# Loads without a waiting chain go from the sync queue to ScalarE's queue, in a two-layer attention and retention trunk

## The chip, the cores and the metric

The kernel runs on one core of a Trainium2 chip. The metric is the device time of one execution in microseconds; the change is judged by it. The core has five engines that run their own instruction streams and meet at semaphores: TensorE (matmuls; PE in the profile, its weight loads PEld), VectorE (DVE), ScalarE (ACT), GpSimd (POOL) and SyncE (SP), which does nothing here but issue DMAs. Data lie in HBM, in SBUF (128 partitions) and, for matmul results, in PSUM.

## The reference

Two layers over one sequence of 2048 tokens, width 1024, then a last RMS norm. Each layer projects the normed input to eight parts of 512 columns, runs chunked attention (8 heads of 64) and chunkwise retention (4 heads of 128) side by side, gates both, and adds the product with `w_out`:

```python
def hybrid_layer(x, norm_gain, w_in, w_out, rel_bias, cos, sin):
    hn = rms_norm(x, norm_gain)
    aq, ak, av, ag, rq, rk, rv, rg = jnp.split(hn @ w_in, cuts, axis=-1)
    ya = chunked_rel_attention(aq, ak, av, rel_bias)      # own chunk of 64 and 8 before, softmax, relative bias
    yr = chunkwise_retention(rq, rk, rv, cos, sin)        # rotary q and k, decay per head, group RMS norm
    y = jnp.concatenate([ya * silu(ag), yr * silu(rg)], axis=-1)
    return x + y @ w_out

def reference(x, positions, norm_gain, w_in, w_out, rel_bias, final_gain):
    cos, sin = rotary_tables(positions, RET_HEAD_DIM)
    for layer in range(DEPTH):                            # DEPTH = 2
        x = hybrid_layer(x, norm_gain[layer], w_in[layer], w_out[layer], rel_bias[layer], cos, sin)
    return rms_norm(x, final_gain)
```

All of it is in float32; the kernel gets there by splitting each operand of a matmul into a float16 high and a float16 low part and adding three products.

## The kernel before

**Tiling.** The 16 token tiles of 128 form four blocks n of 512. The heads form four groups s, each with two attention heads and one retention head. For each layer l, group s and block n the kernel runs `dense_T` (q, k and the rotary q, k of the group, with features on partitions; four outputs j, 24 matmuls each), then `dense_V` (v, rotary v and gates for four token tiles, 24 matmuls each), and beside the dense work of the next block it runs `attention` and `retention` of this one. After the last group of a layer, `wout` multiplies the concatenated y by `w_out` tile by tile, adds x, and in layer 0 also norms the result for layer 1.

**What is written where.** The context `manual_schedule` covers PE, ScalarE, VectorE and GpSimd: their instructions stand in the order in which the Python code calls them. SyncE is not in it, apart from the first block (`sp_order`, left after the first `dense_V`): there the scheduler puts the DMAs in an order of its own, and may move a load ahead of where it is called. A helper `tc.keep_in_program_order` holds one DMA at its place. Each engine works its own list strictly in order: an instruction that waits for a semaphore holds up all that stand behind it.

**Rounds.** `run` steps the dense generators; a round is one step, 8 matmuls of a dense output. In each round it fires what `later(k, fn)` has put k rounds ahead, steps attention, and pulls steps of background work (`bg`, pushed by `push(gen, steps)`): the weights of the next group. Those steps are:

- `prep_T`: loads four sections of `w_in` (1024 x 128, 512 KB each, `load_sec`, tile `stT`) one section ahead, squares each on ScalarE (`sumsq`), finds a power-of-two scale, and converts it to high and low halves. `prep_V` (tile `stV`) and, between the layers, `prep_V_next` do the same for the other four.
- `prep_Omax`: loads the eight blocks of `w_out` (tiles `stO0m`, `stO1m`) and squares each on ScalarE (L312) to find one common scale. Its loop is short:

```python
        for j in range(KT):
            yield
            m1 = sumsq(st, f"{nm}m{j}", None)
            if j + 1 < KT:
                st = load_sec(w_out[l, :, (j + 1) * P:(j + 2) * P], f"{nm}m{j + 1}")
```

- `prep_O`: loads `w_out` again, four sections for each half (tile `stO`), and converts it (L333).

The tiles of `load_sec` come from the pool `w4` with three buffers, so up to three loads can be under way or waiting for their reader.

**Other loads that the change touches.** `tab_load` brings the two rotary tables of a block (`tabc`, `tabs`, 256 KB each) from DRAM, where `tables` has written them once for each block; GpSimd multiplies with them in `turn`. `Sections` loads the retention mask `msk`. `bias_scratch` spreads a head's relative biases over a DRAM scratch (`toep`), and `bias_tiles` reads it back skewed (`bias`), GpSimd and ScalarE (L584) then finish the tile. `y_load` and `x_load` bring a token tile of y and x for `wout`; `y_squares` (L951) is the first reader of y.

**What stays on the sync queue.** The transposes of attention probabilities (`pT<-pq`, L815), on whose result the products with v wait (L823 to L825); the transposes of y and of the normed rows; the copies of q, k and the swapped halves for the rotary product; the stores of y, x and the output. Between `qk` and `pv` of an attention unit lie: VectorE's add and maximum (L807), ScalarE's exponential (L810) and copy (L812), GpSimd's rest (L813), the transpose.

**PSUM.** The dense outputs use the pool `psD` with two buffers, so the third output waits until the first was copied out: for `dense_V` by ScalarE (L763 to L766), then one round later by VectorE (L769 to L773).

Of the kernel before, what the change touches and what calls it, by code (L numbers as in the profile page):

```python
# [18 lines left out]
P = 128  # L19
EPS = 1e-6  # L20
HALF_PI = 1.5707963267948966
RELW = 767
# [5 lines left out]
def hybrid_trunk(ctx: ExitStack, tc: tile.TileContext, x, pos, gain, gcol, w_in, w_out, rel, fgain,  # L28
# [8 lines left out]
    act, dve, pool, pe, sp = nc.scalar, nc.vector, nc.gpsimd, nc.tensor, nc.sync  # L37
# [30 lines left out]
    y_d = [dp.tile([P, D], F32, tag=f"y_d{t}", name=f"y_d{t}") for t in range(NT)]  # L68
    x_d = [dp.tile([P, D], F32, tag=f"x_d{t}", name=f"x_d{t}") for t in range(NT)]
    tab_d = [dp.tile([2, P, 512], F32, tag=f"tab{n}", name=f"tab{n}") for n in range(NS)]  # L70
# [218 lines left out]
    TSEC = (0, 1, 4, 5)  # L289
    VSEC = (2, 6, 3, 7)  # L290

    def load_sec(src, nm, halves=False):

        v = src.rearrange("(k p) c -> p k c", p=P)
        if not halves:
            st = w4.tile([P, KT, P], F32, tag="w4", name=f"st{nm}")
            sp.dma_start(st, v)
            return [(st, 0, KT)]
        h = KT // 2
        st = [b2.tile([P, 3 - i, 512], F16, tag=("rot2", "rot3")[i], name=f"st{nm}_{i}") for i in range(2)]  # L300
        st = [t_[:, 0:2].rearrange("p a c -> p (a c)").bitcast(F32).rearrange("p (k c) -> p k c", c=P) for t_ in st]
        for i in range(2):
            sp.dma_start(st[i], v[:, i * h:(i + 1) * h, :])
        return [(st[i], i * h, (i + 1) * h) for i in range(2)]

    keep = lambda i: i
# [47 lines left out]
    class Sections:  # L354


        def __init__(self, l, s, g, halves=False):
            g.msk = b2.tile([P, P], F32, tag="msk", name=f"msk{l}_{s}")
            sp.dma_start(g.msk, dmask[:, s, :])
            g.rd, g.s = rdc[:, s:s + 1], s  # L360
            self.l, self.s, self.g, self.halves = l, s, g, halves
            self.nm = f"T{l}_{s}"
            self.sts, self.sq, self.iv, self.sv = [], [None] * 4, [None] * 4, [None] * 4
            g.h = b3.tile([P, 4, KT, P], F16, tag="wh", name=f"wh{self.nm}")
            g.l = b3.tile([P, 4, KT, P], F16, tag="wl", name=f"wl{self.nm}")
# [102 lines left out]
    def prep_V_next(l, g):  # L468

        nm = f"V{l}_0"  # L470
        src = [w_in[l, :, VSEC[j] * 512:VSEC[j] * 512 + P] for j in range(4)]
        sts = [load_sec(src[j], f"{nm}{j}", True) for j in range(2)]
        yield
        for j in (2, 3):
            st = b2.tile([P, KT, P], F32, tag="q", name=f"st{nm}{j}")
            sp.dma_start(st, src[j].rearrange("(k p) c -> p k c", p=P))
            sts.append([(st, 0, KT)])
        yield
        g.vh = b3.tile([P, KT, 512], F16, tag="wh", name=f"wh{nm}")
        g.vl = b3.tile([P, KT, 512], F16, tag="wl", name=f"wl{nm}")  # L480
        hi, lo = ([w_[:, :, j * P:(j + 1) * P] for j in range(4)] for w_ in (g.vh, g.vl))
        m = [lowp(sumsq(sts[j], f"{nm}{j}", hi[j]), f"{nm}{j}") for j in range(2)]
        yield
        m2, m3 = (sumsq(sts[j], f"{nm}{j}", hi[j]) for j in (2, 3))
        dve.tensor_tensor(m2, m2, m3, op=ALU.add)
        m.append(lowp(m2, f"{nm}2"))
        yield
        yield
        iv = [None] * 3
        for j in (2, 0, 1):  # L490
            sv, iv[j] = norm_scale(allsum(m[j], f"{nm}{j}"), f"{nm}{j}", gains[l].i)
            for i in ((2, 3) if j == 2 else (j,)):
                yield from convert(sts[i], hi[i], lo[i], sv)
        yield from V_units(l, 0, g, iv, nm)
        g.vdone = 4
# [37 lines left out]
    toep = {}  # L533
    NH = 4 * 2 * DEPTH
    rel_d = dp.tile([NH, RELW + 1], F32, tag="rel_d", name="rel_d")
# [27 lines left out]
    def bias_scratch(l, s):  # L563
        for hh in range(2):
            h = 2 * s + hh
            d = dp.tile([P * RELW], F32, tag=f"toep{h % 4}", name=f"toep{l}_{h}")
            i = sp.dma_start(d.rearrange("(p w) -> p w", w=RELW),
                             rel_d[l * 8 + h:l * 8 + h + 1, 1:RELW + 1].to_broadcast([P, RELW]))
            if (l, s) != (0, 0):
                tc.keep_in_program_order(i)  # L570
            toep[l, h] = d
        yield

    def bias_tiles(l, s, g):

        g.bias = []
        for hh in range(2):
            h = 2 * s + hh
            bt = b3.tile([P, 640], F32, tag="bias", name=f"bias{l}_{h}")
            sp.dma_start(bt, toep[l, h][127:127 + P * (RELW - 1)].rearrange("(p w) -> p w", w=RELW - 1)[:, 0:640])  # L580
            yield
            pool.memset(bt[64:128, 0:64], NEG)
            pool.memset(bt[0:64, 576:640], NEG)
            act.activation(bt, bt, AF.Copy, scale=g.ci[:, 0:1])  # L584
            g.bias.append(bt)
            yield
# [28 lines left out]
    def dense_T(l, s, n, g, st):  # L615
# [4 lines left out]
        def tab_load():  # L620
            while n not in tab_done:
                pull(1)
            sp.dma_start(st.tabc, tab_d[n][0])
            sp.dma_start(st.tabs, tab_d[n][1])

        first = (l, s, n) == (0, 0, 0)

# [297 lines left out]
    def y_load(l, t):  # L925
        u = St()
        u.nm = f"y{l}_{t}"
        u.t = t
        if t < 8:
            u.y = w4.tile([P, D], F32, tag="w4", name=f"yy{u.nm}")  # L930
        else:
            u.y = b2.tile([P, D], F32, tag="q", name=f"yy{u.nm}")
        sp.dma_start(u.y, y_d[t])
        return u

    def x_load(l, u):
        if l + 1 == DEPTH or u.t < 12:
            f = (hT[l, 0] if l + 1 == DEPTH else hT_of(l + 1, NS - 1))[u.t // 2 % 2].rearrange("p k c -> p (k c)").bitcast(F32)
            u.x = f[:, u.t % 2 * D:(u.t % 2 + 1) * D]
        else:  # L940
            u.x = w4.tile([P, D], F32, tag="w4", name=f"xx{u.nm}")
        sp.dma_start(u.x, x[u.t * P:(u.t + 1) * P, :] if l == 0 else x_d[u.t])

    def y_squares(l, u):
        u.m = b2.tile([P, 1], F32, tag="ym", name=f"ym{u.nm}")
# [213 lines left out]
    def norms_from_input(ts, spaces, rows, tab):  # L1159

        def load(k):
            u = us[k]
            u.x = spaces[k] if spaces else w4.tile([P, D], F32, tag="w4", name=f"xin{u.t}")
            if not spaces:
                sp.dma_start(u.x, x[u.t * P:(u.t + 1) * P, :])

        def sq(k):
            u = us[k]
# [21 lines left out]
        for t in ts:  # L1190
            u = St()
# [172 lines left out]
    for l in range(DEPTH):  # L1364
        gO = [Grp(), Grp()]
        go = Grp()
        for s in range(NSW):
            g = grp(l, s)
            for n in range(NS):
                first = (l, s, n) == (0, 0, 0)  # L1370
                if not first:
                    st = St()
# [4 lines left out]
                if n == 0 and not first:  # L1377
                    bs, bt = bias_scratch(l, s), bias_tiles(l, s, g)
                    later(1, lambda bs=bs: next(bs))
                    for k in (4, 8, 17, 21):  # L1380
                        later(k, lambda bt=bt: next(bt))
                if (l, s) == (0, 0) and 0 < n < NS - 1:
                    if n == 1:
# [30 lines left out]
                run(dense_V(l, s, n, g, st), att, 24 if n == NS - 1 and s < NSW - 1 else 12)  # L1414
                if first:
                    sp_order.__exit__(None, None, None)
                if att[0] is not None:
                    drain(att[0])
                att = [attention(l, s, n, g, st, states.get((l, s, n - 1)))]
# [84 lines left out]
```

## Time and profile before

| | us |
|---|---|
| median of three runs | 2087.54 |
| lowest and highest | 2083.29, 2090.22 |
| the profiled execution | 2084.99 |
| its span, first to last instruction | 2083.2 |
| TensorE busy | 2008.0 (96%) |
| VectorE busy | 1245.1 (60%) |
| ScalarE busy | 1141.9 (55%) |
| GpSimd busy | 679.1 (33%) |

All DMAs that the program issues itself are issued by SyncE: 645504 packets, 311.12 MB, and their time takes 66.0% of the span of 16 DMA engines. Busy time doesn't count the issuing of DMAs or waiting. In the lists of waits a row names the waiting engine, what it was about to write and the line, then what released it, and the total, the number and the longest of these waits. "SPq" rows are the sync queue's own waits. In the timelines a row has start, duration, engine, line, operation, out<-in by the program's names; in square brackets the engine's idle time just before and what ended it. In the list of DMA issues the last number is the median time from issue to landing.

### The profile page before, as it was taken

The page shows a single profiled execution, that of the slowest core. Times are in us where ns is not written, and L with a number is a line of the kernel's source. Part 1 is how long each engine was busy: PE and PEld are TensorE (multiplying, and loading weights), DVE is VectorE, ACT ScalarE, POOL GpSimd, SP SyncE. Part 2 cuts the span into 40 slices and gives each one's busy share as a digit, 9 for nine tenths or more (in the row PEclk, how much of TensorE's full clock was granted, in tenths as well). Part 3 has the DMA queues.
Part 4 walks back from the last instruction along what each step waited for, and adds up shares of the span by engine and source line. Part 5 has one row for each costly group of instructions (what it writes and reads, how often), then busy time and mean ns, then how long its engine had stood idle before and what let it go on. Part 6 is the DMA issues. An engine that isn't in the chain of part 4 may idle for free.

```text
span 2083.2 us, 39398 instructions
## 1 busy us (share of the span) xinstructions
PE 2008.0 (96%) x14014; PEld 1051.6 (50%) x14014; DVE 1245.1 (60%) x3817; ACT 1141.9 (55%) x2530; POOL 679.1 (33%) x701
## 2 busy tenths in 40 slices
PE   6988999999999999998999999999999999999998
PEld 4444555555555555544444555555555555554543
DVE  7776666556556655676653656565655566557643
ACT  7556665456565654554444546554655665446432
POOL 0234343444344434330003343434243334333100
PEclk9999999999999999999999999999999999999999
DMA  8768675547575754799774547555655867548974
GB/s 233 166 152 172 143 164 106 117 112 158 114 185 118 158 141 102 158 227 259 200 188 98 124 102 147 119 124 102 142 119 125 182 145 166 122 102 192 213 197 126
DMA packets 645701, 313.63 MB, mean 151 GB/s; under 512 B 459232, under 2 KB 602080, under 8 KB 645504
## 3 DMA queue, kind: packets, MB, share of 16 engines
q1 hardware_dynamic: 645504, 311.12, 66.0%
q8 instruction: 109, 1.79, 0.4%
q14 instruction: 88, 0.72, 0.1%
HBM read 123.26 MB, written 41.98 MB: 79 GB/s over the span
## 4 chain that ended last, share of the span: by engine, by line
PE 48%; DMA 3%; POOL 1%; issue 1%; DVE 1%; ACT 1%; SPq 0%; POOLq 0%; ACTq 0%; DVEq 0%
PE dT L736 14%; PE dV L755 14%; PE dO L1098 13%; DMA pT<-pq 2%; PE r L857 2%; PE S L804 1%; PE S L803 1%; PE o L823 1%; PE o L824 1%; PE o L825 1%; DMA toep<-rel_d 0%; POOL pq L813 0%; PE ptn L999 0%; DMA stO1m<-in_w_out_dram 0%; ACT sc L810 0%
## 5 line engine op out<-in xcount | busy, mean ns | idle before, releaser
L813 POOL TENSOR_TENSOR pq<-sc,pq 128x640 f16<-128x640 f32 (+4 forms) x256 | 319.9, 1250 | 894.6 <-ACT pq L812 479.7
L810 ACT ACTIVATE sc<-sc,mq,cT 128x640 f32<-128x640 f32 (+4 forms) x256 | 218.5, 853 | 623.8 <-DVE rl L829 324.3
L736 PE MATMUL dT<-hTh,whT 128*128 128x512 f16 x1008 | 350.4, 383 | 5.0 <-DMA hTh<-xa 2.2
L755 PE MATMUL dV<-whV,hTh 128*128 128x512 f16 x1024 | 353.1, 381 | 1.7 <-DVE gt L773 1.3
L755 PE MATMUL dV<-wlV,hTh 128*128 128x512 f16 x1024 | 353.0, 380 | 0.0
L755 PE MATMUL dV<-whV,hTl 128*128 128x512 f16 x1024 | 352.8, 380 | 0.0
L736 PE MATMUL dT<-hTl,whT 128*128 128x512 f16 x1008 | 348.4, 381 | 0.0
L736 PE MATMUL dT<-hTh,wlT 128*128 128x512 f16 x1008 | 348.1, 380 | 0.0
L755 PEld LDWEIGHTS <-hTh 128*128 128x128 f16 x2048 | 196.5, 98 | 217.0 <-DVE gt L773 3.8
L736 PEld LDWEIGHTS <-whT 128*128 128x128 f16 x2016 | 193.1, 98 | 217.8 <-issue 12.9
L807 DVE CUSTOM_DVE_ANT_0 sc<-S,bias 128x640 f32<-128x640 f32 (+4 forms) x256 | 188.4, 736 | 125.3 <-PE S L804 124.6
L1098 PE MATMUL dO<-whO,yhy 128*128 128x512 f16 x512 | 194.6, 380 | 1.0 <-DMA yhy<-hTh 0.8
L1098 PE MATMUL dO<-whO,yly 128*128 128x512 f16 x512 | 194.3, 380 | 1.2 <-DMA yly<-hTl 0.6
L1098 PE MATMUL dO<-wlO,yhy 128*128 128x512 f16 x512 | 194.4, 380 | 0.0
L812 ACT ACTIVATE pq<-sc 128x640 f16<-128x640 f32 (+4 forms) x256 | 171.5, 670 | 8.1
L1098 PEld LDWEIGHTS <-yhy 128*128 128x128 f16 x1024 | 99.8, 98 | 116.1 <-DMA yhy<-hTh 1.3
L755 PEld LDWEIGHTS <-hTl 128*128 128x128 f16 x1024 | 99.2, 98 | 110.8 <-issue 1.7
L736 PEld LDWEIGHTS <-wlT 128*128 128x128 f16 x1008 | 97.5, 98 | 112.9 <-issue 6.2
L823 PE MATMUL o<-v,pT 128*128 128x65 f16 x1120 | 130.5, 194 | 15.6 <-DMA pT<-pq 15.5
L803 PE MATMUL S<-k,q 128*128 128x128 f16 (+3 forms) x592 | 143.6, 269 | 0.0
L823 PEld LDWEIGHTS <-pT 128*128 128x128 f16 x1120 | 106.0, 97 | 53.0 <-DMA pT<-pq 24.4
L804 PE MATMUL S<-k,q 128*128 128x128 f16 (+3 forms) x592 | 131.0, 269 | 0.0
(352 smaller groups left out, 3497.3 us busy)
## 6 DMA issues: line engine op xcount, KB each, us to landing
q<-qq SPq DMA_DIRECT2D x128, 128.0 KB, 2.5
yyy<-y_d SPq DMA_DIRECT2D x32, 512.0 KB, 4.9
stT<-in_w_in_dram SPq DMA_DIRECT2D x27, 512.0 KB, 5.0
stV<-in_w_in_dram SPq DMA_DIRECT2D x26, 512.0 KB, 4.5
k<-kk SPq DMA_DIRECT2D x128, 64.0 KB, 2.0
swp<-rot SPq DMA_DIRECT2D x64, 128.0 KB, 2.7
tabc<-tab SPq DMA_DIRECT2D x32, 256.0 KB, 2.7
tabs<-tab SPq DMA_DIRECT2D x32, 256.0 KB, 3.1
```

The costliest lines, as they stand in the source:

```text
L736: pe.matmul(ps, w_[:, j, kt, :], h_[:, kt, :], start=(m == 0), stop=(m == 23))
L755: pe.matmul(ps, h_[:, kt, a * P:(a + 1) * P], w_[:, kt, :], start=(m == 0), stop=(m == 23))
L803: pe.matmul(o, st.q[:, hx, 0, cs], k_, start=True, stop=False)
L804: pe.matmul(o, st.q[:, hx, 1, cs], k_, start=False, stop=True)
L807: dve.tensor_tensor_reduce(out=v, in0=S[:, 0:w], in1=g.bias[hx][:, 640 - w:640], scale=1.0, scalar=-3.0e38, op0=ALU.add, op1=ALU.max, accu ...
L810: act.activation(v, v, AF.Exp, bias=m[:, 0:1], scale=g.c[:, 0:1])
L812: act.activation(pq[:, 0:w], v, AF.Copy)
L813: pool.tensor_tensor(pq[:, w:2 * w], v, pq[:, 0:w], op=ALU.subtract)
L823: pe.matmul(o[:, 0:65], u.p[:, b, :], v_[:, 0:65], start=(b == 0), stop=False)
L824: pe.matmul(o[:, 0:64], u.p[:, b, :], v_[:, 65:129], start=False, stop=False)
L857: pe.matmul(out_, w_, m_, start=(i == 0), stop=(i + 1 == len(pairs)))
L1098: pe.matmul(ps, h_[:, kt, :], w_[:, kt, :], start=(m == 0), stop=(m == 23))
```

## The change

A new function `bring` issues a DMA on the engine that `bulk["e"]` names. This is the sync engine until the end of the first block's `dense_V`, and ScalarE from there on. The loads of weight sections, masks, Toeplitz scratch, bias tiles, rotary tables, y, x and later input tiles use it: 259 DMAs move to ScalarE's own queue. Because ScalarE is under the manual schedule, they stand there in the order of the calls. The scratch loads lose their `keep_in_program_order`, and the four steps of `bias_tiles` come 6, 10, 19 and 22 rounds after the group's start instead of 4, 8, 17 and 21. The number of instructions and the tiles are the same.

```diff
@@ -289,18 +289,24 @@
     TSEC = (0, 1, 4, 5)
     VSEC = (2, 6, 3, 7)
 
+    bulk = {"e": sp}
+
+    def bring(dst, src):
+
+        return bulk["e"].dma_start(dst, src)
+
     def load_sec(src, nm, halves=False):
 
         v = src.rearrange("(k p) c -> p k c", p=P)
         if not halves:
             st = w4.tile([P, KT, P], F32, tag="w4", name=f"st{nm}")
-            sp.dma_start(st, v)
+            bring(st, v)
             return [(st, 0, KT)]
         h = KT // 2
         st = [b2.tile([P, 3 - i, 512], F16, tag=("rot2", "rot3")[i], name=f"st{nm}_{i}") for i in range(2)]
         st = [t_[:, 0:2].rearrange("p a c -> p (a c)").bitcast(F32).rearrange("p (k c) -> p k c", c=P) for t_ in st]
         for i in range(2):
-            sp.dma_start(st[i], v[:, i * h:(i + 1) * h, :])
+            bring(st[i], v[:, i * h:(i + 1) * h, :])
         return [(st[i], i * h, (i + 1) * h) for i in range(2)]
 
     keep = lambda i: i
@@ -356,7 +362,7 @@
 
         def __init__(self, l, s, g, halves=False):
             g.msk = b2.tile([P, P], F32, tag="msk", name=f"msk{l}_{s}")
-            sp.dma_start(g.msk, dmask[:, s, :])
+            bring(g.msk, dmask[:, s, :])
             g.rd, g.s = rdc[:, s:s + 1], s
             self.l, self.s, self.g, self.halves = l, s, g, halves
             self.nm = f"T{l}_{s}"
@@ -473,7 +479,7 @@
         yield
         for j in (2, 3):
             st = b2.tile([P, KT, P], F32, tag="q", name=f"st{nm}{j}")
-            sp.dma_start(st, src[j].rearrange("(k p) c -> p k c", p=P))
+            bring(st, src[j].rearrange("(k p) c -> p k c", p=P))
             sts.append([(st, 0, KT)])
         yield
         g.vh = b3.tile([P, KT, 512], F16, tag="wh", name=f"wh{nm}")
@@ -564,10 +570,8 @@
         for hh in range(2):
             h = 2 * s + hh
             d = dp.tile([P * RELW], F32, tag=f"toep{h % 4}", name=f"toep{l}_{h}")
-            i = sp.dma_start(d.rearrange("(p w) -> p w", w=RELW),
-                             rel_d[l * 8 + h:l * 8 + h + 1, 1:RELW + 1].to_broadcast([P, RELW]))
-            if (l, s) != (0, 0):
-                tc.keep_in_program_order(i)
+            bring(d.rearrange("(p w) -> p w", w=RELW),
+                  rel_d[l * 8 + h:l * 8 + h + 1, 1:RELW + 1].to_broadcast([P, RELW]))
             toep[l, h] = d
         yield
 
@@ -577,7 +581,7 @@
         for hh in range(2):
             h = 2 * s + hh
             bt = b3.tile([P, 640], F32, tag="bias", name=f"bias{l}_{h}")
-            sp.dma_start(bt, toep[l, h][127:127 + P * (RELW - 1)].rearrange("(p w) -> p w", w=RELW - 1)[:, 0:640])
+            bring(bt, toep[l, h][127:127 + P * (RELW - 1)].rearrange("(p w) -> p w", w=RELW - 1)[:, 0:640])
             yield
             pool.memset(bt[64:128, 0:64], NEG)
             pool.memset(bt[0:64, 576:640], NEG)
@@ -620,8 +624,8 @@
         def tab_load():
             while n not in tab_done:
                 pull(1)
-            sp.dma_start(st.tabc, tab_d[n][0])
-            sp.dma_start(st.tabs, tab_d[n][1])
+            bring(st.tabc, tab_d[n][0])
+            bring(st.tabs, tab_d[n][1])
 
         first = (l, s, n) == (0, 0, 0)
 
@@ -930,7 +934,7 @@
             u.y = w4.tile([P, D], F32, tag="w4", name=f"yy{u.nm}")
         else:
             u.y = b2.tile([P, D], F32, tag="q", name=f"yy{u.nm}")
-        sp.dma_start(u.y, y_d[t])
+        bring(u.y, y_d[t])
         return u
 
     def x_load(l, u):
@@ -939,7 +943,7 @@
             u.x = f[:, u.t % 2 * D:(u.t % 2 + 1) * D]
         else:
             u.x = w4.tile([P, D], F32, tag="w4", name=f"xx{u.nm}")
-        sp.dma_start(u.x, x[u.t * P:(u.t + 1) * P, :] if l == 0 else x_d[u.t])
+        bring(u.x, x[u.t * P:(u.t + 1) * P, :] if l == 0 else x_d[u.t])
 
     def y_squares(l, u):
         u.m = b2.tile([P, 1], F32, tag="ym", name=f"ym{u.nm}")
@@ -1162,7 +1166,7 @@
             u = us[k]
             u.x = spaces[k] if spaces else w4.tile([P, D], F32, tag="w4", name=f"xin{u.t}")
             if not spaces:
-                sp.dma_start(u.x, x[u.t * P:(u.t + 1) * P, :])
+                bring(u.x, x[u.t * P:(u.t + 1) * P, :])
 
         def sq(k):
             u = us[k]
@@ -1377,7 +1381,7 @@
                 if n == 0 and not first:
                     bs, bt = bias_scratch(l, s), bias_tiles(l, s, g)
                     later(1, lambda bs=bs: next(bs))
-                    for k in (4, 8, 17, 21):
+                    for k in (6, 10, 19, 22):
                         later(k, lambda bt=bt: next(bt))
                 if (l, s) == (0, 0) and 0 < n < NS - 1:
                     if n == 1:
@@ -1414,6 +1418,7 @@
                 run(dense_V(l, s, n, g, st), att, 24 if n == NS - 1 and s < NSW - 1 else 12)
                 if first:
                     sp_order.__exit__(None, None, None)
+                    bulk["e"] = act
                 if att[0] is not None:
                     drain(att[0])
                 att = [attention(l, s, n, g, st, states.get((l, s, n - 1)))]
```

## The prediction

> **What bounds the kernel now.** I read the page's head first, then the windows, the waits of TensorE and of the sync queue, the DMA issues, and last the timelines of ScalarE, VectorE and TensorE where the moved loads are used.
>
> ```profile
> span 2083.2 us, 39398 instructions
> PE 2008.0 (96%) x14014; PEld 1051.6 (50%) x14014; DVE 1245.1 (60%) x3817; ACT 1141.9 (55%) x2530; POOL 679.1 (33%) x701
> ```
> ```profile
> 596.00:619.00 23.00, 21.72 (x162) 11.33 (x160) 11.39 (x45) 19.31 (x46) 9.08 (x9) 1.00 0.90 221
> ...
> 856.00:1075.00 219.00, 207.51 (x1223) 102.83 (x1222) 138.78 (x346) 115.33 (x213) 35.89 (x36) 0.99 0.90 218
> ...
> 1614.00:1637.00 23.00, 21.46 (x160) 11.13 (x158) 11.77 (x46) 18.91 (x46) 9.05 (x8) 1.00 0.89 223
> ```
>
> TensorE is the bound: 2008.0 of 2083.2 us, so 75 us is all that any change of queues can win. ScalarE is 55% busy over the span, but the columns of the windows (start:end, length, then busy time of PE, PEld, DVE, ACT, POOL, granted clock, DMA share, GB/s) say that the mean hides something: in the two 23 us in which `prep_Omax` squares W_out, ScalarE is busy for 19.31 and 18.91 us, 84% and 82%. It has some 4 us to spare there. The granted clock is full in these rows and explains nothing.
>
> What the sync queue costs TensorE today:
>
> ```profile
> PEld L823 <- DMA pT<-pq: 24.4, 18, 3.8
> ...
> PE o L823 <- DMA pT<-pq: 15.5, 14, 3.3
> ```
> ```profile
> SPq L580 <- DMA toep<-rel_d: 28.0, 7, 4.6
> ```
> ```profile
> 1480.48 5.18 DMA toep<-rel_d
> 1486.82 8.11 DMA pT<-pq
> ```
>
> TensorE stood 15.5 us, at 14 places, for transposed probabilities. Seven times the sync queue stood for a Toeplitz scratch to land before it could issue the bias load (28.0 us together), with a transpose behind it; the chain of waits shows one such pair, at 1480 and 1487 us. This is what the change can win.
>
> **What is removed from the sync queue: a gain of 13 us.** 259 loads leave it, the waits on the scratch with them. I take nearly the whole 15.5 us of the pT waits as gone, less what transfers still collide: 13. The ends are 0 (a load already under way is on the same DMA engines) and 24, what the weight loads of the same matmuls waited, part of it beside running matmuls.
>
> The Trainium skill, page "DMA: Bandwidth & Descriptors", section "Issuing engines are not separate DMA queues", speaks against more: loads from either queue run on the same 16 DMA engines, and a second issuer saves issue time only. By that rule the gain would come from issue alone, below my 13; no row of before has a load on a second queue, so the trace leaves it open.
>
> **What is added: loads in ScalarE's written order.** The sync engine's order is left to the scheduler, which issues a load as soon as its buffer is free. ScalarE's order is written by hand. So each load now stands where the code calls it, and what ScalarE computes from it stands shortly behind, in the same in-order queue. The issue itself (about 0.4 to 0.5 us, rows below) is small; the landing is not.
>
> ```profile
> 545.94 0.53 SPq L297 DMA_DIRECT2D stO0m<-in_w_out_dram  x1
> ...
> 557.61 0.38 SPq L297 DMA_DIRECT2D stO0m<-in_w_out_dram  x1
> ```
> ```profile
> yyy<-y_d SPq DMA_DIRECT2D x32, 512.0 KB, 4.9
> stT<-in_w_in_dram SPq DMA_DIRECT2D x27, 512.0 KB, 5.0
> stV<-in_w_in_dram SPq DMA_DIRECT2D x26, 512.0 KB, 4.5
> ...
> stO<-in_w_out_dram SPq DMA_DIRECT2D x16, 512.0 KB, 4.9
> ```
> ```profile
> DMA to landing us min/median/max: 4.0/4.9/6.0
> ```
>
> (The last row is that of tile stO0m.) The first W_out block was issued at 545.94 us and squared at 597.22, 51 us later. In the changed program the listing of ScalarE's instructions has it directly ahead of the square.
>
> **prep_Omax, twice: a loss of 46 us.** ScalarE's timeline before:
>
> ```profile
> 597.22 1.04 ACT L312 ACTIVATE stO0m<-stO0m 128x1024 f32<-128x1024 f32 x1
> 598.17 0.19 ACT L312 ACTIVATION_READ_ACCUMULATOR stO0m<-stO0m 128x1 f32 x1
> ...
> 599.26 1.04 ACT L312 ACTIVATE stO0m<-stO0m 128x1024 f32<-128x1024 f32 x1
> ...
> 601.58 1.05 ACT L312 ACTIVATE stO0m<-stO0m 128x1024 f32<-128x1024 f32 x1
> ...
> 604.98 0.92 ACT L810 ACTIVATE sc<-sc,mq,cT 128x640 f32<-128x640 f32 x1 [2.26 <-DVE mq L809]
> ...
> 606.58 1.04 ACT L312 ACTIVATE stO0m<-stO0m 128x1024 f32<-128x1024 f32 x1
> ...
> 608.34 1.04 ACT L312 ACTIVATE stO0m<-stO0m 128x1024 f32<-128x1024 f32 x1
> ...
> 610.49 1.04 ACT L312 ACTIVATE stO0m<-stO0m 128x1024 f32<-128x1024 f32 x1
> ...
> 613.04 0.92 ACT L810 ACTIVATE sc<-sc,mq,cT 128x640 f32<-128x640 f32 x1 [0.90 <-DVE mq L809]
> ...
> 614.64 1.04 ACT L312 ACTIVATE stO0m<-stO0m 128x1024 f32<-128x1024 f32 x1
> ...
> 616.22 1.06 ACT L312 ACTIVATE stO0m<-stO0m 128x1024 f32<-128x1024 f32 x1
> ```
>
> Load j+1 is called right behind square j. Each square with its read-out takes 1.13 us, so the work that lies between a load and its square is the distance of two squares less 1.13 and less idle time: 0, 0.9, 1.2, 1.6, 0.6, 1.0, 2.1 and 0.45 us, 7.9 together. A landing takes 4.0 to 4.9 us; I take 4.5, since a waiting ScalarE leaves the DMA engines emptier. The waits are 8 x 4.5 - 7.9 = 28.1 us per layer. Two things cover some of it: the idle 2.26 + 0.90 in these rows, and TensorE's lead.
>
> ```profile
> 601.99 0.41 DVE L773 SCALAR_TENSOR_TENSOR gt<-gt,dV 128x256 f32<-128x256 f32 x1
> ```
> ```profile
> 604.56 0.38 PE L755 MATMUL dV<-whV,hTh 128*128 128x512 f16 x1
> ```
>
> The PSUM buffer of a `dense_V` block was cleared at 602.40 (VectorE's rest follows ScalarE's copies at once), and TensorE began to fill it again at 604.56: a lead of 2.2 us, which I use as the lead everywhere. Queued behind ScalarE's waiting squares are just these PSUM copies and the exponentials of attention; TensorE has two dense buffers and can go no further. So TensorE loses 28.1 - 3.2 - 2.2 = 22.7 us per layer, 46 in all. With landings of 4.0 it is 37, with 4.9 it is 52.
>
> **The first rotary table for block 1: 6.5 us.**
>
> ```profile
> 95.49 0.59 SPq L128 DMA_DIRECT2D tab<-xa  x1
> ```
> ```profile
> 89.57 1.28 ACT L810 ACT_TABLE_LOAD   x1 [1.59 <-DVE mq L809]
> ```
> ```profile
> tab<-xa SPq DMA_DIRECT2D x8, 64.0 KB, 2.0
> ```
>
> `tab_load` for n = 1 comes right after the switch of queues and reads what the sync queue is still writing. The last write is issued at 95.49 and lands 2.0 later; with two issues ScalarE is free at about 98.3 where it went on at 89.57: 8.7 late, less the lead, 6.5 (0 to 9).
>
> **First sections of prep_T, six times: 11 us.**
>
> ```profile
> 316.05 1.04 ACT L312 ACTIVATE whT<-stT 128x1024 f16<-128x1024 f32 x1
> ...
> 318.06 0.60 ACT L638 ACTIVATE qq<-dT 128x512 f16<-128x512 f32 x1 [0.88 <-PE dT L736]
> ```
>
> Load 0 and its square fall into neighbouring rounds here: 5.0 less 0.88 idle less the lead is 1.9, six times 11 (0 to 20). Sections 1 to 3 are loaded one section ahead, with a whole section's squares, scales and conversions between, and cost nothing.
>
> **The other moved loads.**
>
> ```profile
> 868.36 0.26 ACT L763 ACTIVATE v<-dV 128x128 f16<-128x128 f32 x1
> ...
> 869.49 1.13 ACT L333 ACTIVATE whO<-stO,o_s 128x1024 f16<-128x1024 f32 x1
> ```
> ```profile
> 1980.33 1.15 ACT L226 ACTIVATE hTh<-yyy,sy 128x1024 f16<-128x1024 f32 x1 [4.68 <-DVE iy L145]
> ```
>
> `prep_O`, four groups: between its first load and the conversion stand the copies of one `dense_V` block, 1.1 us (869.49 - 868.36). So 4.9 - 1.1 - 2.2 = 1.6, and half of it again for the third section, which is also called late: 9 us (0 to 20). First loads of `prep_V`, late in five of six groups, with as little between: 4.5 - 1.1 - 2.2 = 1.2 each, 6 us (0 to 15). Output stage of layer 0: `y_load` stands half a tile ahead of its square, and half-sections of layer 1 are issued there too; TensorE is idle for 11.5 us of this stage already (219.00 - 207.51), so it has no lead to give. I take 1 us for each of ten tiles, 10 us (0 to 25). In layer 1's output stage ScalarE idles 4.7 us in each tile and hides it: nothing. x loads are used by VectorE a tile later: nothing. Masks, scratch and bias (its steps come 2, 2, 2 and 1 rounds later, for this distance) keep away from their use: nothing.
>
> **A wait that the change adds.** In the built program every DMA signals one of eight semaphores in turn and waits for the DMA before on the same one. A load on ScalarE therefore waits for one of the sync queue, often issued just before, with ScalarE's whole order behind it. The landings of before say that nearly all of these are over in time; only the table loads of block 0 in six groups stand close behind a store. I take 2 us (0 to 12, that is 2 us for each of the six).
>
> **Sum.** 46 + 6.5 + 11 + 9 + 6 + 10 + 2 - 13 = 77.5 us. The profiled execution took 2085.0 us (span 2083.2), 2.5 under the median of 2087.5; 2085.0 + 77.5 + 2.5 = 2165 us. Lowest terms with the largest gain: 37 - 24 = +13, 2100 us. Highest with no gain: 52 + 9 + 20 + 15 + 20 + 25 + 12 = +153, 2240 us.
>
> **Rivals.**
>
> ```profile
> L815 SPq DMA_TRANSPOSE pT<-pq x256: 1167/1322/4108, 80.8 to 1952.5; - x128
> ```
> ```profile
> L312 ACT ACTIVATE whV<-stV 128x1024 f16<-128x1024 f32 (+1 forms) x30 | 29.6, 986 | 2.1 <-PE dO L1098 2.1
> ```
>
> *Faster:* ScalarE's waits stay under its idle time, and TensorE loses its pT waits. The mechanism is that a wait of up to 5 us falls where ScalarE would wait for VectorE anyway; it decides where ScalarE idles over 5 us per load. For it: 45% idle overall. Against it: the 84% in `prep_Omax`. It would give 2087.5 - 15.5 = 2072. The Trainium skill has a rule on this side (same page, "Queues, rings and completion order"): each DMA engine takes turns between queue rows by packet, so a transpose on one row need not queue behind a load on another. Chance 0.08. *No change,* gain and waits cancelling: 0.03. *Only prep_Omax counts:* the lead covers single waits of 5 us, 2087.5 + 37 - 24 to + 46 - 13, 2100 to 2120: 0.17. *The two queues hold each other up:* ScalarE late makes the sync queue late through the shared semaphores, and loads issue behind a transpose's 1.3 us instead of 0.5. 259 x 0.8 = 207 us of ScalarE's time, half of it on the path, gives 2165 + 100 = 2265: 0.14. *My forecast:* 0.58. The Trainium skill's table "Rules for kernel authors" on the same page says to issue a load early and wait late; this agrees with the forecast, and the 51 us above against none is what it means here.
>
> **Numbers.** Below 0.3% this kernel's runs can't tell a change. Faster 0.08, same 0.03, slower 0.89. The range 2100 to 2240 leaves out the first two and most of the fourth.
>
> **What would show it.** Right: in the windows of `prep_Omax` (by then 23 us longer each) ScalarE's L312 on stO0m waits 3 to 5 us for "DMA stO0m" eight times and TensorE idles for ScalarE or VectorE; idle before L312 on the stV sections, 2.1 us now, at 10 or more; pT waits of the sync queue behind a scratch gone. Wrong: if those L312 waits are there and TensorE is still 96% busy, the lead was deeper than 2.2 us; if L312 waits are absent, loads land sooner than 4 us; if TensorE's new idle time names pT or swp, the queues hold each other up.

## The result, and the profile after

The changed kernel takes 2163.2 us (median of 4 runs, 2161.9 to 2167.7) against 2085.4 us before on the same chip: 1.038 times, 95% interval 1.0345 to 1.0414, so 78 us slower. Forecast were 2165 us, and slower. The profiled execution took 2167.7 us.

The page of the changed kernel: span, busy time, and the queues (packets, MB, share of 16 engines' span). Here q1 carries what SyncE issues, and q10 what ScalarE issues.

```profile
span 2165.9 us, 39273 instructions
...
PE 2028.8 (94%) x14014; PEld 1055.7 (49%) x14014; DVE 1235.5 (57%) x3817; ACT 1144.1 (53%) x2530; POOL 676.3 (31%) x701
...
q1 hardware_dynamic: 530128, 202.52, 46.0%
q10 hardware_dynamic: 115376, 108.60, 18.4%
```

A third of the bytes left the sync queue. TensorE is 20.8 us longer busy with the same 14014 matmuls (2028.8 against 2008.0), and 137 us idle instead of 75. What waits now (engine, line waited at, what ended the wait: us in total, times, longest; L312 of before is L318 here, L333 is L339, L823 is L827, L857 is L861):

```profile
PE r L861 <- ACT dT L865: 28.4, 6, 7.6
...
ACT whO L339 <- DMA stO<-in_w_out_dram: 21.6, 10, 3.9
...
PE r L861 <- DVE dT L869: 21.2, 15, 3.4
...
ACT whT L318 <- DMA stT<-in_w_in_dram: 20.4, 6, 5.0
...
PEld L827 <- DMA pT<-pq: 18.9, 16, 2.9
...
ACT stO1m L318 <- DMA stO1m<-in_w_out_dram: 17.4, 6, 5.8
...
ACT stO0m L318 <- DMA stO0m<-in_w_out_dram: 16.4, 6, 4.8
...
PE o L827 <- DMA pT<-pq: 11.9, 9, 2.4
...
ACT rhy L955 <- DMA yyy<-y_d: 10.4, 6, 6.2
...
ACT L814 <- DMA tab<-xa: 9.3, 1, 9.3
...
ACT whV L318 <- DMA stV<-in_w_in_dram: 7.9, 5, 1.8
```

ScalarE now stands for weights at every place that loads them. TensorE's longest waits have a new name: not a DMA, but the small copy `dT` of retention that stands in ScalarE's order (28.4 us; the waits of before have 4.7 for it). In four of the six, 20 us together, it stands behind a waiting square of `prep_Omax`; the longest, 7.6 us, is behind the wait for the first rotary table. Waits for transposed probabilities fell only from 15.5 to 11.9 us. Windows of the changed kernel over the eight squares of `prep_Omax` in each layer, and over TensorE's work in the output stage of layer 0 (start:end, length, busy PE, PEld, DVE, ACT, POOL, granted clock, DMA share, GB/s):

```profile
612.30:652.00 39.70, 25.08 (x157) 12.65 (x155) 12.70 (x52) 21.42 (x50) 8.40 (x8) 0.83 0.60 134
1677.70:1715.00 37.30, 26.12 (x164) 12.92 (x165) 15.67 (x63) 20.29 (x47) 10.38 (x9) 0.81 0.51 119
```
```profile
929.00:1119.00 190.00, 166.24 (x924) 79.44 (x923) 107.95 (x260) 84.28 (x143) 21.52 (x25) 0.98 1.01 213
```

The work of some 160 matmuls that took 23 us before takes 39.7 and 37.3 us, at a granted clock of 0.83 and 0.81 where it was 1.00. ScalarE's timeline at four of these squares and loads, and TensorE's beside them (start, us, what, and in brackets the idle time before it):

```profile
614.26 1.06 ACT L318 ACTIVATE stO0m<-stO0m 128x1024 f32<-128x1024 f32 x1 [4.85 <-DMA stO0m<-in_w_out_dram]
...
618.59 1.06 ACT L318 ACTIVATE stO0m<-stO0m 128x1024 f32<-128x1024 f32 x1 [2.17 <-DMA stO0m<-in_w_out_dram]
618.60 0.37 ACTq L296 DMA_DIRECT2D stO0m<-in_w_out_dram  x1
...
622.90 1.06 ACT L318 ACTIVATE stO0m<-stO0m 128x1024 f32<-128x1024 f32 x1 [1.87 <-DMA stO0m<-in_w_out_dram]
622.91 0.38 ACTq L296 DMA_DIRECT2D stO0m<-in_w_out_dram  x1
...
627.44 1.06 ACT L318 ACTIVATE stO0m<-stO0m 128x1024 f32<-128x1024 f32 x1
```
```profile
621.09 0.39 PE L861 MATMUL r<-rv,dT 128*128 128x128 f16 x2 [4.77 <-ACT dT L865]
...
624.78 0.29 PE L861 MATMUL r<-rv,dT 128*128 128x128 f16 x1 [2.98 <-DVE dT L869]
...
625.18 0.63 PE L759 MATMUL dV<-whV,hTh 128*128 128x512 f16 x1
625.60 0.63 PE L759 MATMUL dV<-whV,hTl 128*128 128x512 f16 x1
...
630.64 0.38 PE L759 MATMUL dV<-wlV,hTh 128*128 128x512 f16 x1
630.86 0.38 PE L759 MATMUL dV<-whV,hTh 128*128 128x512 f16 x1
```

The squares follow each other by one landing, 4.3 us (622.90 - 618.59). The next load is issued at the *start* of a square (618.60), not behind its end. TensorE pauses for 4.8 and 3.0 us, and then its 512-column matmuls start 0.42 us apart (625.60 - 625.18) until they are back at 0.22 (630.86 - 630.64).

To see where time is lost I laid the start times of the same matmuls of both kernels side by side, from one profiled execution each. The offset of the changed kernel grows by 18 us at `prep_Omax` of layer 0, 19 in layer 1, 19 in the output stage of layer 0 and 9 in that of layer 1, by 10 at the first rotary table (of which it has lost 7 again by 180 us), by 6 at the first section of the first `prep_T`, and by less at some other places; it shrinks by about 3 and 6 us near 1290 and 1500 us of the kernel before, two places where before the sync queue stood for a Toeplitz scratch.

### The profile page after: what moved, and what is told of

It reads as the page before. It is cut to its first block, busy times and chain, and to the rows that moved or that the text cites. A ratio compares the mean times of both kernels' runs of the same rounds, so it can differ in the third digit from the quotient of the medians.

```text
span 2165.9 us, 39273 instructions
## 1 busy us (share of the span) xinstructions
PE 2028.8 (94%) x14014; PEld 1055.7 (49%) x14014; DVE 1235.5 (57%) x3817; ACT 1144.1 (53%) x2530; POOL 676.3 (31%) x701
## 5 line engine op out<-in xcount | busy, mean ns | idle before, releaser
L740 PEld LDWEIGHTS <-whT 128*128 128x128 f16 x2016 | 193.7, 99 | 222.8 <-issue 20.4
L807 PE MATMUL S<-k,q 128*128 128x128 f16 (+3 forms) x592 | 143.0, 268 | 2.9 <-DVE mq L811 2.9
L827 PE MATMUL o<-v,pT 128*128 128x65 f16 x1120 | 130.8, 194 | 11.9 <-DMA pT<-pq 11.9
L914 POOL TENSOR_TENSOR rss<-rss,mhalf 128x1 f32<-128x1 f32 x128 | 72.7, 568 | 193.7 <-DVE rss L913 168.0
L828 PE MATMUL o<-v,pT 128*128 128x64 f16 x1120 | 131.0, 196 | 0.0
```

What stands on the lines that cost most here:

```text
L740: pe.matmul(ps, w_[:, j, kt, :], h_[:, kt, :], start=(m == 0), stop=(m == 23))
L807: pe.matmul(o, st.q[:, hx, 0, cs], k_, start=True, stop=False)
L827: pe.matmul(o[:, 0:65], u.p[:, b, :], v_[:, 0:65], start=(b == 0), stop=False)
L828: pe.matmul(o[:, 0:64], u.p[:, b, :], v_[:, 65:129], start=False, stop=False)
L914: pool.tensor_tensor(ss, ss, mhalf, op=ALU.pow)
```

## The experiments

Every ratio is to the kernel before, run on the same chip, with its 95% interval; 1% is 20.9 us. The times of different groups of runs are compared by these ratios.

**prep_Omax back on the sync queue, and prep_Omax alone on ScalarE.** The first undoes one part of the change, the second does that part alone on the kernel before:

```diff
 # after, with prep_Omax's loads on the sync queue
-        st = load_sec(w_out[l, :, 0:P], f"{nm}m0")
+        st = load_sec(w_out[l, :, 0:P], f"{nm}m0", q=sp)
-                st = load_sec(w_out[l, :, (j + 1) * P:(j + 2) * P], f"{nm}m{j + 1}")
+                st = load_sec(w_out[l, :, (j + 1) * P:(j + 2) * P], f"{nm}m{j + 1}", q=sp)
 # before, with only these two lines changed: q=act
```

> As the changed kernel, but the 16 loads of prep_Omax go back to the sync queue. Theory (ScalarE stands before a square until the load called just ahead of it has landed): the changed kernel's matmuls fell 18 and 20 us further behind at these two places, so 2163 - 38 = 2125 us, and the idle time before L318 on stO0m and stO1m (16.4 and 17.4 us) is gone. Rival (issue time on ScalarE and the semaphores that the two queues share; every moved load costs alike): 16 of 259 loads go back, 6% of 78 us, 2158 us.

> As the kernel before, but the 16 loads of prep_Omax alone are issued by ScalarE, where they are called. Theory: the whole cost of this part is there, 2085 + 38 = 2123 us (37 to 52 over the kernel before by the prediction's terms). Rival (each moved load costs alike): 2085 + 5 = 2090 us.

Measured: 2126.8 us, ratio 1.019 (1.0176 to 1.0211), and 2122.1 us, 1.0174 (1.016 to 1.0188). The part is worth 39 us out of the changed kernel (1.0379 - 1.0193) and 36 us alone. Waits of the kernel with only this part:

```profile
ACT stO0m L312 <- DMA stO0m<-in_w_out_dram: 16.2, 7, 4.8
ACT stO1m L312 <- DMA stO1m<-in_w_out_dram: 15.9, 7, 4.2
```

Sixteen loads of 259 make half of the loss, with the same waits as in the whole change. This is shown from both sides.

**prep_Omax on ScalarE, called three blocks ahead.** Same queue, another distance:

```diff
-        st = load_sec(w_out[l, :, 0:P], f"{nm}m0")
+        ld = lambda j: load_sec(w_out[l, :, j * P:(j + 1) * P], f"{nm}m{j}")
+        sts = [ld(j) for j in range(3)]
         for j in range(KT):
             yield
-            m1 = sumsq(st, f"{nm}m{j}", None)
-            if j + 1 < KT:
-                st = load_sec(w_out[l, :, (j + 1) * P:(j + 2) * P], f"{nm}m{j + 1}")
+            m1 = sumsq(sts[j], f"{nm}m{j}", None)
+            if j + 3 < KT:
+                sts.append(ld(j + 3))
```

> As the changed kernel, with all loads on ScalarE's queue, but prep_Omax calls each W_out block three squares ahead (its three buffers allow it) instead of one. Theory: distance is what counts, not the queue. Only the first square of a layer still stands 4 to 5 us, of which 2 us are covered; so 6 of the 38 us stay, 2163 - 32 = 2131 us. Rival (the queue or the issue time is the cost): no change, 2163 us.

Measured: 2139.7 us, 1.026 (1.0229 to 1.029), 25 us less than the changed kernel, where 32 were expected.

```profile
ACT stO0m L318 <- DMA stO0m<-in_w_out_dram: 5.5, 3, 4.3
...
ACT stO1m L318 <- DMA stO1m<-in_w_out_dram: 4.5, 1, 4.5
```

Of 16.4 and 17.4 us of waits, 5.5 and 4.5 are left, mostly the first block's, whose load is still called right ahead of its square. So the distance between call and use costs, not ScalarE as an issuer. The steps of TensorE at these places fell from 18 and 19 us to 8 and 6.

**Only scratch and bias loads on ScalarE.** Of the change, only the 28 loads that ended SyncE's scratch waits, with the later steps of the bias tiles:

```diff
-            i = sp.dma_start(d.rearrange("(p w) -> p w", w=RELW), ...)
-            if (l, s) != (0, 0):
-                tc.keep_in_program_order(i)
+            (sp if (l, s) == (0, 0) else act).dma_start(d.rearrange("(p w) -> p w", w=RELW), ...)
...
-            sp.dma_start(bt, toep[l, h]...)
+            (sp if (l, s) == (0, 0) else act).dma_start(bt, toep[l, h]...)
...
-                    for k in (4, 8, 17, 21):
+                    for k in (6, 10, 19, 22):
```

> As the kernel before, but only the Toeplitz scratch and the bias tiles (28 loads) are issued by ScalarE, with the later steps of the change. Theory: this is the part that wins. The sync queue's 28.0 us of waiting for a scratch are gone, ScalarE waits for nothing new, and TensorE loses about half of its 15.5 us of pT waits: 2085 - 7 = 2078 us, between 2070 and 2085. Rival (the transposes wait for GpSimd and for transfers, not for the queue): 2085 us, no change.

Measured: 2078.7 us, 0.9967 (0.9955 to 0.9978). This version beats both kernels. SyncE's wait for the scratch, 28.0 us before, is down to one entry:

```profile
SPq L657 <- DMA toep<-rel_d: 0.2, 1, 0.2
```

The offset against before falls by about 4 us near 1290 and 6 near 1500 us, the same two places at which the changed kernel gained.

**The later bias steps alone, all on the sync queue:**

```diff
-                    for k in (4, 8, 17, 21):
+                    for k in (6, 10, 19, 22):
```

> The kernel before with the bias tiles' steps later alone (6, 10, 19, 22 for 4, 8, 17, 21); scratch and bias loads stay on the sync queue in their order. Theory (the gain of 7 us of the version with only these loads moved is the queue's: SyncE no longer waits for the scratch): 2083 to 2086 us. Rival (the later steps bring it): 2077 to 2080 us.

Measured: 2087.0 us, 1.0003 (0.9993 to 1.0012), nothing. SyncE still waits:

```profile
SPq L580 <- DMA toep<-rel_d: 26.2, 7, 4.1
```

So the gain of 7 us doesn't come from the later steps; it comes with the move to the other queue. The scratch loads also lost their fixed place in the sync queue's order, and that alone, without the move, wasn't tried.

**The issues without the landings.** In the kernel before, all loads stay on the sync queue; at each place where the changed kernel issues a load, ScalarE issues an extra 8 KB transfer to DRAM that nothing reads:

```diff
+        if bulk["e"] is act:
+            bulk["n"] = bulk.get("n", 0) + 1
+            act.dma_start(dp.tile([P, 16], F32, tag=f"dummy{bulk['n'] % 8}", ...), x[0:P, 0:16])
+        return sp.dma_start(dst, src)
```

> As the kernel before, with all loads on the sync queue, but wherever the changed kernel issues a load on ScalarE, ScalarE issues a DMA of 8 KB to a DRAM scratch that nobody reads (259 of them; nothing is taken from the result). It measures issue time on ScalarE and the shared semaphores without the wait for a landing. Theory: some 110 us of issue time lie under ScalarE's idle time, 2085 to 2095 us. Rival (issue and semaphores are the cost): most of the 78 us, 2140 us or more.

Measured: 2099.8 us, 1.0074 (1.0048 to 1.0101), 15 us: between the two, nearer the theory. ScalarE waits before issues:

```profile
ACT sc L819 <- DMA dummy<-in_x_dram: 23.9, 7, 8.0
```

259 more issues on ScalarE's queue are not free, but they are a fifth of the loss. Two things blur this number: the eight buffers of the dummies are themselves reused, and the transfers come on top of the others.

**The y loads back on the sync queue, and prep_O back on the sync queue** (each is the changed kernel with one edit):

```diff
-        bring(u.y, y_d[t])
+        sp.dma_start(u.y, y_d[t])
```
```diff
-        sts = [load_sec(w_out[l, :, c * 512:c * 512 + P], f"{nm}0")]
+        sts = [load_sec(w_out[l, :, c * 512:c * 512 + P], f"{nm}0", q=sp)]
 # and the same for sections 1 to 3
```

> As the changed kernel, but the 32 loads of y go back to the sync queue. Theory: the changed kernel's matmuls fell 17 us behind in layer 0's output stage and 3 in layer 1's; the y loads are the most of it, the half-sections of layer 1 the rest. 2163 - 13 = 2150 us. Rival (the stage suffers from crowded DMA engines, not from the order): 2163 us.

> As the changed kernel, but the 16 loads of prep_O go back to the sync queue. Theory: the four steps of the delay where prep_O runs (2.4, 4.7, 4.3 and 6.2 us) are theirs, 2163 - 17 = 2146 us. The prediction had 9 us for them: 2154. Rival (the steps come from attention's transposes there): 2163 us.

Measured: 2161.1 us, 1.035 (1.0319 to 1.0378), and 2172.5 us, 1.0415 (1.039 to 1.0439). The first is what the rival expected, so y alone is not the cause; the second is slower than both theories had it, and its interval overlaps that of the changed kernel. In the second the wait itself went as foreseen, from 21.6 to

```profile
ACT whO L339 <- DMA stO<-in_w_out_dram: 4.6, 2, 2.7
```

and the steps of TensorE near 744 and 1762 us (times of the kernel before) with it, but as much was lost near 690 to 700, at 1705 and in the output stage of layer 0, where the offset now grows by 26 us instead of 19. A wait that goes is not yet time that is won.

**The output stage's own loads back on the sync queue:** y, x and the sections loaded in two halves, in the changed kernel; four later input tiles of the first group go back with them.

```diff
-        bring(u.y, y_d[t])
+        sp.dma_start(u.y, y_d[t])
-        bring(u.x, x[u.t * P:(u.t + 1) * P, :] if l == 0 else x_d[u.t])
+        sp.dma_start(u.x, x[u.t * P:(u.t + 1) * P, :] if l == 0 else x_d[u.t])
-            bring(st[i], v[:, i * h:(i + 1) * h, :])
+            sp.dma_start(st[i], v[:, i * h:(i + 1) * h, :])
-                bring(u.x, x[u.t * P:(u.t + 1) * P, :])
+                sp.dma_start(u.x, x[u.t * P:(u.t + 1) * P, :])
```

> The changed kernel with the loads of the output stage itself back on the sync queue: y, x, and the sections loaded as two halves. Theory (these loads together, not y alone, cost the 17 us that layer 0's output stage lost): 2145 to 2150 us. Rival (the stage lags for what happens elsewhere, the queue's order or the sections of the next layer): 2158 to 2166 us.

Measured: 2147.6 us, 1.030 (1.0284 to 1.0314), 17 us less. Windows over the same matmuls, first of this kernel, then of the kernel before:

```profile
933.00:1104.00 171.00, 162.37 (x916) 79.24 (x914) 105.78 (x249) 81.25 (x140) 22.26 (x25) 0.99 0.93 218
```
```profile
894.00:1065.00 171.00, 163.30 (x926) 80.61 (x925) 106.36 (x251) 82.41 (x143) 22.51 (x25) 0.99 0.90 218
```

171 us both, where the changed kernel has 190. So these loads together cost the 17 us (19 by the windows); with y alone back the offset still grew by 15 us over this stage. Whether x or the halves matter more wasn't tried. The parts don't stand alone: with `prep_Omax` back on the sync queue the same stage lost 26 us.

**Only loads that are used late.** The changed kernel with `prep_Omax`, `prep_O`, y, halves and the tables of the first group on the sync queue; 177 transfers stay on ScalarE:

```diff
-            bring(st.tabc, tab_d[n][0])
-            bring(st.tabs, tab_d[n][1])
+            q = sp if (l, s) == (0, 0) else act
+            q.dma_start(st.tabc, tab_d[n][0])
+            q.dma_start(st.tabs, tab_d[n][1])
 # and the edits above for prep_Omax, prep_O, y and the halves
```

> As the changed kernel, but every load that proved to stand close ahead of its use goes back to the sync queue: prep_Omax, prep_O, y, half-sections, the rotary tables of group 0 of layer 0. ScalarE keeps 159 or more loads that are called well ahead. Theory: the parts add up, 38 + 17 + 13 + 7 + about 4 for the half-sections are gone; 5 us of the first prep_T sections stay and 8 us of the scratch are won: 2084 us, 2078 to 2092. Rival (the two queues hold each other up in proportion to the loads moved): 2163 - 78 x 90/259 = 2136 us.

Measured: 2106.3 us, 1.0097 (1.0075 to 1.0118): a miss by 22 us. ScalarE's, SyncE's and TensorE's timelines at the largest step that is left (TensorE loses 6.3 us):

```profile
695.79 0.36 ACTq L628 DMA_DIRECT2D tabc<-tab  x1
700.15 0.33 ACTq L629 DMA_DIRECT2D tabs<-tab  x1
700.58 0.92 ACT L815 ACTIVATE sc<-sc,mq,cT 128x640 f32<-128x640 f32 x1 [6.32 <-DMA y_d<-yr]
```
```profile
694.58 0.54 SPq L921 DMA_DIRECT2D y_d<-yr  x1
695.23 1.34 SPq L820 DMA_TRANSPOSE pT<-pq  x1
```
```profile
704.49 0.10 PEld L828 LDWEIGHTS <-pT 128*128 128x128 f16 x1 [3.86 <-DMA pT<-pq]
```

Between two table issues ScalarE stands 4 us, and what ends this is a store of y on the other queue, with which a table load has no data in common. The store was issued just before, at 694.58. This is the shared semaphore of the prediction, seen at work: ScalarE is idle for 6.3 us before the exponential behind it, against 3.8 before the same one in the kernel before. What holds TensorE up here came another way, though: its next weights, in the last row, wait for a transpose that was issued at 695.23, so that ScalarE had done its part before the table issues, and that landed 9 us later, beside the table load. So this place shows the stand of ScalarE, but not that the stand is what costs.

**The rest in two halves.** On the version with only scratch and bias loads on ScalarE: besides these the whole sections of `prep_T`, `prep_V` and `prep_V_next`; or the rotary tables and masks behind group 0.

```diff
 # sections
-            sp.dma_start(st, v)
+            (q or bulk["e"]).dma_start(st, v)      # bulk["e"] is act behind the first block; prep_Omax, prep_O: q=sp
 # tables and masks
-            sp.dma_start(st.tabc, tab_d[n][0])
-            sp.dma_start(st.tabs, tab_d[n][1])
+            q = sp if (l, s) == (0, 0) else act
+            q.dma_start(st.tabc, tab_d[n][0])
+            q.dma_start(st.tabs, tab_d[n][1])
-            sp.dma_start(g.msk, dmask[:, s, :])
+            (sp if (l, s) == (0, 0) else act).dma_start(g.msk, dmask[:, s, :])
```

> The kernel before with the bias loads on ScalarE (2078.7 us), and besides these the whole weight sections of prep_T and prep_V behind group 0 on ScalarE, each still called one step ahead of its Square; prep_Omax, prep_O, tables, y and x loads stay on the sync queue. Theory (a load called one step ahead makes ScalarE wait for its landing): the first sections' waits of 3 to 5 us come back as in the changed kernel and reach TensorE in part, 2090 to 2098 us. Rival (what costs beside prep_Omax is the completion semaphores that the two queues share, by the number of transfers): some 50 more transfers at 0.14 us, 2086 us or less.

> The kernel before with the bias loads on ScalarE (2078.7 us), and besides these the rotary tables and the masks of all groups behind group 0: 63 transfers more, which no ScalarE instruction reads soon. Theory (landings cost, and these are read late): 2079 to 2083 us. Rival (shared semaphores: a table's issue on ScalarE waits for a store of the sync queue to land, 4 us at 700 us in an earlier run): 2088 to 2096 us, with ScalarE standing before table issues that start as a sync transfer lands.

Measured: sections 2091.0 us, 1.0027 (1.0017 to 1.0038), which is 12.5 us over the version without them (1.0027 - 0.9967) and in the theory's range. Tables 2084.8 us, 0.9997 (0.9986 to 1.0009), 6 us over that version: between theory (0 to 4) and rival (9 to 17).

With the sections, ScalarE's waits come back as foreseen, but most of them cost TensorE nothing:

```profile
ACT whT L314 <- DMA stT<-in_w_in_dram: 20.6, 6, 5.9
...
ACT whV L314 <- DMA stV<-in_w_in_dram: 9.6, 6, 2.0
```
```profile
1699.20 6.15 SPq L815 DMA_TRANSPOSE pT<-pq  x1
...
1709.54 0.20 PE L823 MATMUL o<-v,pT 128*128 128x65 f16 x1 [3.81 <-DMA pT<-pq]
```

Matmul by matmul against the version without them, TensorE loses 4 to 5 us at the first of the six `prep_T` waits and 2 at the fourth. At the other four, each of some 3 us, and at the first sections of `prep_V` it loses under 0.4 us each. The largest step, 6 us, is at 1700 to 1710 us: there a transpose takes 6.15 us to issue and lands 10 us after its start, with two scratch loads and a section of ScalarE's and a section of SyncE's in flight. In the version without the sections on ScalarE the same transpose was issued in 2.5 us.

With the tables, nearly the whole 6 us are one step, at 1108 to 1113 us. The rows are the swapped copies of the rotary product without the tables on ScalarE; then, with them, SyncE's wait; then the same copies, and who waits for them:

```profile
1096.72 1.50 SPq L671 DMA_DIRECT2D swp<-rot  x1
```
```profile
SPq L658 <- DMA hTh<-rhn: 3.5, 1, 3.5
```
```profile
1103.69 0.46 SPq L672 DMA_DIRECT2D swp<-rot  x1
1110.61 0.63 ACT L681 ACTIVATE rot<-rot 128x512 f16<-128x512 f32 x1 [11.66 <-POOL rot L678]
1112.99 0.39 PE L754 MATMUL dV<-whV,hTh 128*128 128x512 f16 x1 [4.32 <-DVE gt L772]
```

Here SyncE stands, not ScalarE: before a copy of k it waits 3.5 us for a transpose of normed rows that shares its semaphore and none of its data. This transpose landed 8.5 us after its issue, with two table loads of ScalarE in flight; without them it took 3.8 us. The swapped copies behind it come 6 to 7 us later, GpSimd and ScalarE wait for them, and the PSUM buffer that TensorE needs is cleared late. Loads that nobody waits for can cost too, when they fall beside the other queue's short transfers. Both places are from one profiled execution each.

## Why the prediction was right, point by point

Total and sign came out, 2165 against 2163, and the main mechanism with them: ScalarE waits for loads that its written order calls too late. That the total is right to 2 us is luck; the terms came out less evenly. By the ratios the 78 us are: `prep_Omax` 36 to 39, loads of the output stage 17, sections of `prep_T` and `prep_V` 12.5, tables and masks 6, scratch and bias -7. These add up to 65 to 68. The remaining 10 to 13 lie in `prep_O`, the first group's tables, and in what parts cost only together; the runs didn't split them. The version with late loads only says as much: its parts (sections, tables, bias) make 11.5 us, and it measured 20 over the kernel before; its x loads weren't measured alone. The prediction also put layer 1's output stage at nothing, while the offset grows by 9 us there in the profiled execution; 5 to 7 of them stay whichever part goes back to the sync queue. Why is open.

- **prep_Omax, 46 predicted, 36 to 39 measured.** Place and mechanism are right, the working is not. The waits are 16.4 and 17.4 us, six of 1.8 to 5.8 us in each layer, not 28.1 in eight of 3 to 5: the prediction let a landing begin when a square with its read-out ends, but the load is issued when the square starts, so that about 1.2 us of each landing is covered by the square itself. Against this, nothing of what should have covered the waits did: idle time of 0.9 to 2.0 us for VectorE is still there between the squares, and TensorE lost 18 and 19 us, more than ScalarE waited. Part of that is a cost that the sum had no term for, the slow matmuls behind each pause (2.5 us in the first layer's window, 12 of them at 0.21 us extra). Two errors of opposite sign.
- **Tables of the first group, 6.5 predicted.** ScalarE was to go on at 98.3 us; its next instruction starts at 98.68, behind the 9.3 us wait in the list above. TensorE's offset grows by 10 us there, to 11; it is 6 at 140 us and 4 at 180. No run undid this part alone.
- **Sections of prep_T and prep_V, 11 + 6 predicted, 12.5 measured.** The size came near by luck. The six first sections wait as said, 20.4 us, but the step to TensorE fails: 1.9 us from each were predicted, and in four of the six, with waits of some 3 us, TensorE loses 0.2 us at most. There it has lead enough for such a wait, so 2.2 us was too little to use everywhere. The waits of `prep_V` cost nothing that can be seen either; in the run that measured 12.5 us nearly half of it is the slow transpose above. The group of `prep_V` squares, idle 2.1 us before, has:

```profile
L318 ACT ACTIVATE whV<-stV 128x1024 f16<-128x1024 f32 (+1 forms) x30 | 29.6, 988 | 12.4 <-DMA stV<-in_w_in_dram 7.9 <-PE dO L1102 4.5
```

- **Output stage of layer 0, 10 predicted, 17 measured.** Right that TensorE has no lead there. Wrong in naming y: that load alone back on its queue brought nothing that can be told from none, all of the stage's loads together brought 17 us.
- **prep_O, 9 predicted.** Not settled: its wait of 21.6 us is there, but without it the kernel is no faster.
- **Gain of the sync queue, 13 predicted, 7 measured.** Only the scratch waits were worth something. TensorE's waits for transposes stayed at 11.9 of 15.5 us: a transpose takes its 3.0 us from issue to landing (median of 256) in both kernels, and those over 6 us have become more, 21 for 6. The page "DMA: Bandwidth & Descriptors" of the Trainium skill, section "Issuing engines are not separate DMA queues", says that a second issuer saves issue time only, which the prediction took to mean less than 13. The measured 7 us are less, but they don't test that rule: what ended there was SyncE's wait for a landing, 28.0 us, and not issue time alone.
- **Shared semaphores, 2 predicted.** Too low: 15 us for the 259 unread transfers, and up to 6 for the tables, where a late landing had its part. That "only the table loads of block 0 in six groups stand close behind a store" named the right place for ScalarE's stand; the costly one in the run with the tables, at 1108 us, was SyncE's, and in the run with late loads only TensorE's largest step ends with a slow transpose. The rival of 100 us for it is out.
- **The rivals.** "Only prep_Omax" falls, since 39 us are left when it is undone. "Faster" holds for 28 loads of 259.

## What to carry to other kernels

A load that moves from a queue whose order a scheduler sets to an engine whose order is written by hand loses its lead: look up how long ahead it was issued, and call it at least one landing earlier, or leave it. Count also whose completion its issue waits for, above all on an engine that sits in the chain of the bound, and look which short transfers of the other queue it will run beside. Move first the few loads whose own waits block a queue; here 28 of 259 held the whole gain that was shown.

## What the runs showed of the hardware that was not expected

A pause costs TensorE more than its length. After the 4.8 and 3.0 us pauses shown above, 512-column matmuls start 0.42 us apart for about 5 us and then 0.22 again; the granted clock is 0.50 between 621 and 630 us, and 0.83 and 0.81 over the windows of `prep_Omax`. Counted over 512-column matmuls alone, 112 in the whole span have their successor at 0.39 to 0.46 us in the changed kernel, 49 in the kernel before, 37 in the one with only the bias loads moved: 63 more at 0.21 us are 13 of the 78 us, spread over the parts above. The Trainium skill, page "TensorE: Matmul & The Clock Gate", Part 1, states a gate that halves the clock after idle and reopens it after some microseconds of sustained work; the trace agrees, and the prediction had left it out.
